# Moving and holding back the first tile's two stores in a streaming GELU-times kernel

## The chip, the cores and the metric

The kernel runs on one core of a Trainium2 chip. The metric is the device time of one execution in microseconds (us). Before the change it is 469.45 us, the median of 3 runs (469.33 to 469.8).

## The reference

The input is `x`, float32, of shape 32 × 512 × 2048. Each row of 2048 is cut in two halves of 1024: the first half goes through the exact GELU, and the result is multiplied by the second half.

```python
x1, x2 = (x[..., :half_dim].copy(), x[..., half_dim:].copy())
gelu_x1 = 0.5 * x1 * (1 + erf(x1 / np.sqrt(2)))
return (gelu_x1 * x2).astype(np.float32)
```

So 134.2 MB are read and 67.1 MB are written, and there is one activation and one product for every element of the output.

## The kernel before

The 16384 rows are cut into 16 tiles. A tile gives each of the 128 partitions 8 consecutive rows (R = 8), so a tile's load is 8 MB, 64 KB for each partition, and its store 4 MB, 32 KB for each partition. There are two input buffers and two output buffers, used in turn by even and odd tiles.

Four engines take part. SyncE only issues transfers: all the loads (line 47), and at the end the stores of tiles 14 and 15. ScalarE computes the GELU of a piece of a tile (line 81) and issues the other stores (line 54). VectorE multiplies the piece in place in the output buffer by the second half (line 89). Transfers issued by SyncE stand in one queue (q1 in the profile), those issued by ScalarE in another (q10); both are served by the same 16 DMA engines.

The order is written out by hand, with semaphores. Before the loop SyncE issues the two halves of tile 0 (rows 0 to 3 and 4 to 7, one semaphore each) and all of tile 1. In the loop:

- Tiles 0 and 15 are worked on in pieces of 2, 2 and 4 rows, all others in pieces of 5 and 3 rows (line 74). ScalarE waits for the tile's input before its first piece, and VectorE waits for each GELU (line 87).
- Every load of a tile and every store of the tile two before it count up the same semaphore, `ready[k]`, so ScalarE's first piece of tile i waits both for the load of tile i and for the store of tile i − 2, whose output buffer it will overwrite (line 79).
- A store waits until the products that it needs are counted in `mul_done` (line 52). The store of tile 0 is in two halves of 4 rows (2 MB each), issued by ScalarE after the second and after the third piece (line 101). Tile 15's is in two halves too, issued by SyncE. The others are whole (lines 103 to 106).
- After the products of tile i, SyncE issues the load of tile i + 2 into the buffer that has come free (lines 107 to 109).

A wait on an engine holds everything behind it on that engine: a store that ScalarE issues waits in ScalarE's own instruction order.

Of the kernel before, what the change touches and what calls it, by code (L numbers as in the profile page):

```python
# [1 line left out]

# [4 lines left out]

GELU = mybir.ActivationFunctionType.Gelu


@with_exitstack
def kernel(
    ctx: ExitStack,
    tc: tile.TileContext,
    x: bass.AP,
    out: bass.AP,
):
    nc = tc.nc
    P = nc.NUM_PARTITIONS

    x_flat = x.flatten_outer_dims()
    out_flat = out.flatten_outer_dims()
    n_rows, dim = x_flat.shape
    half = dim // 2

    R = 8
    x_t = x_flat.rearrange("(n p r) d -> n p r d", p=P, r=R)
    o_t = out_flat.rearrange("(n p r) d -> n p r d", p=P, r=R)
    n_tiles = x_t.shape[0]
    x_bufs = [nc.alloc_sbuf_tensor(f"x{k}_tile", [P, R, dim], x.dtype) for k in range(2)]  # L30
    o_bufs = [nc.alloc_sbuf_tensor(f"o{k}_tile", [P, R, half], out.dtype) for k in range(2)]

    first = [nc.alloc_semaphore(f"first{j}") for j in range(2)]
    ready = [nc.alloc_semaphore(f"ready{k}") for k in range(2)]
    gelu_done = nc.alloc_semaphore("gelu_done")
    mul_done = nc.alloc_semaphore("mul_done")
    tail_stored = nc.alloc_semaphore("tail_stored")
    n = {sem.name: 0 for sem in [*first, *ready, gelu_done, mul_done, tail_stored]}  # L40

    def counted(ins, sem, by):
        ins.then_inc(sem, by)
        n[sem.name] += by

    def load(i, rows, sem):
        ins = nc.sync.dma_start(out=x_bufs[i % 2][:, rows, :], in_=x_t[i][:, rows, :])  # L47
        counted(ins, sem, 16)
        return ins

    def store(queue, i, rows, sem):
        queue.wait_ge(mul_done, n[mul_done.name])
        counted(
            queue.dma_start(out=o_t[i][:, rows, :], in_=o_bufs[i % 2][:, rows, :]), sem, 16
        )

    for ins in (  # L60
        load(0, slice(0, 4), first[0]),
        load(0, slice(4, 8), first[1]),
        load(1, slice(0, 8), ready[1]),
    ):
        tc.no_tile_sem_insts.add(ins.ins.name)
    tc.close()
    tc.compile()  # L67

    for i in range(n_tiles):
        k = i % 2  # L70
        last = i == n_tiles - 1
        pieces = i == 0 or last
        steps = ((0, 2), (2, 4), (4, 8)) if pieces else ((0, 5), (5, 8))
        for lo, hi in steps:
            rows = slice(lo, hi)
            if i == 0 and lo % 4 == 0:
                nc.scalar.wait_ge(first[lo // 4], 16)
            elif lo == 0:
                nc.scalar.wait_ge(ready[k], n[ready[k].name])
            counted(  # L80
                nc.scalar.activation(  # L81
                    out=o_bufs[k][:, rows, :], in_=x_bufs[k][:, rows, :half], func=GELU
                ),
                gelu_done,
                1,
            )
            nc.vector.wait_ge(gelu_done, n[gelu_done.name])
            counted(
                nc.vector.tensor_mul(  # L89
                    out=o_bufs[k][:, rows, :],  # L90
                    in0=o_bufs[k][:, rows, :],
                    in1=x_bufs[k][:, rows, half:],
                ),
                mul_done,
                1,
            )
            if pieces and hi % 4 == 0:
                if last:
                    store(nc.sync, i, slice(hi - 4, hi), tail_stored)
                else:  # L100
                    store(nc.scalar, i, slice(hi - 4, hi), ready[k])
        if not pieces:
            if i == n_tiles - 2:
                store(nc.sync, i, slice(0, R), tail_stored)
            else:
                store(nc.scalar, i, slice(0, R), ready[k])
        if i + 2 < n_tiles:
            nc.sync.wait_ge(mul_done, n[mul_done.name])
            load(i + 2, slice(0, R), ready[k])


    nc.scalar.drain()  # L112
    for sem in (*first, *ready):
        nc.scalar.sem_clear(sem)
    nc.vector.drain()
    nc.vector.sem_clear(gelu_done)
    nc.sync.sem_clear(mul_done)
    nc.sync.wait_ge(tail_stored, n[tail_stored.name]).then_inc(
        tail_stored, -n[tail_stored.name]
    )  # L120


# [1 line left out]
_INS = ['x']  # L124
_OUTS = [((32, 512, 1024), 'float32')]


# [23 lines left out]
```

## Time and profile before

| | |
|---|---|
| time, median of 3 runs | 469.45 us (469.33 to 469.8) |
| span of the profiled execution | 467.9 us |
| VectorE busy | 140.5 us (30%), 34 instructions |
| ScalarE busy | 115.5 us (25%), 35 instructions |
| read and written | 134.22 MB and 67.11 MB, 430 GB/s over the span |
| transfers on SyncE's queue (q1) | 2880 packets, 142.61 MB |
| transfers on ScalarE's queue (q10) | 2160 packets, 58.72 MB |

The profile is of one execution, whose own time is not given apart from its span; the median of the runs lies 1.55 us above that span, for what goes on before the first and after the last recorded instruction. The page gives busy shares by engine, then the span in 40 slices, where a digit is the busy share in tenths (9 is 90% or more). A DMA queue's share is the time that its packets took, as a share of the span of all 16 engines. A line such as `47.20 4.48 ACT o_tile L81` of the chain gives the start, the duration, the engine, what it wrote, and the line of the kernel. `ACT <- DMA` in the list of waits reads: ScalarE waited for a transfer; the numbers are the sum, the count and the longest. ACTq and SPq are the engines' instruction queues, where transfers are issued.

### The profile page before, as it was taken

To read this page: it belongs to the slowest core of one execution; us is meant where nothing else is said; L and a number is where in the kernel's file an instruction comes from. 1 tells how busy PE (TensorE), PEld (TensorE's weight loads), DVE (VectorE), ACT (ScalarE), POOL (GpSimd) and SP (SyncE) were. 2 spreads that over 40 slices of the span, in tenths; PEclk is the share of its full clock that TensorE was granted. 3 is DMA by queue.
4 is the path that set the end of the run, shared out by engine and by line. 5 is a ranking of instruction groups with operands and counts; after the bars stand their busy time and mean duration, and the time that the engine had idled before them with its cause. 6 is when DMAs were issued, how large, how long until landed. Compare 5 with 4: busy or idle time off the path is not lost.

```text
span 467.9 us, 152 instructions
## 1 busy us (share of the span) xinstructions
DVE 140.5 (30%) x34; ACT 115.5 (25%) x35; POOL 0.2 (0%) x4
## 2 busy tenths in 40 slices
DVE  0330514207052060511606116060150702507043
ACT  1320606042060410604106050050500506014060
POOL 0000000000000000000000000000000000000000
DMA  8999999999999999999999999999999999999998
GB/s 359 448 448 443 403 405 492 409 403 448 459 437 403 434 417 493 403 403 448 476 420 403 445 406 493 403 406 445 487 409 403 445 451 448 403 434 417 493 389 373
DMA packets 5041, 201.34 MB, mean 430 GB/s; under 512 B 560, under 2 KB 560, under 8 KB 560
## 3 DMA queue, kind: packets, MB, share of 16 engines
q1 hardware_dynamic: 2880, 142.61, 70.6%
q10 hardware_dynamic: 2160, 58.72, 29.1%
q14 instruction: 1, 0.01, 0.0%
HBM read 134.22 MB, written 67.11 MB: 430 GB/s over the span
## 4 chain that ended last, share of the span: by engine, by line
DMA 76%; DVE 14%; ACT 8%; ACTq 0%; SPq 0%; issue 0%
DMA out_dram<-o_tile 66%; DVE o_tile L89 14%; DMA x_tile<-in_x_dram 10%; ACT o_tile L81 8%; ACTq L112 0%; SPq L47 0%
## 5 line engine op out<-in xcount | busy, mean ns | idle before, releaser
L89 DVE TENSOR_TENSOR o_tile<-o_tile,x_tile 128x5120 f32<-128x5120 f32 (+3 forms) x34 | 140.5, 4171 | 319.7 <-ACT o_tile L81 319.7
L81 ACT ACTIVATE o_tile<-x_tile 128x5120 f32<-128x5120 f32 (+3 forms) x34 | 114.3, 3407 | 337.4 <-DMA out_dram<-o_tile 301.6
L81 ACT ACT_TABLE_LOAD x1 | 1.3, 1283 | 2.9 <-PEq L67 2.9
L135 POOL MEMSET const-bfloat16-1.0<- 128x1 bf16 x1 | 0.1, 101 | 0.0
L135 POOL MEMSET const-uint8-127<- 128x1 uint8 x1 | 0.1, 101 | 0.0
L135 POOL MEMSET const-float32-0.0<- 128x1 f32 x1 | 0.1, 98 | 0.2 <-issue 0.2
L135 POOL MEMSET const-float32-1.0<- 128x1 f32 x1 | 0.1, 98 | 0.0
## 6 DMA issues: line engine op xcount, KB each, us to landing
out_dram<-o_tile ACTq DMA_DIRECT2D x13, 4096.0 KB, 44.7
x_tile<-in_x_dram SPq DMA_DIRECT2D x2, 4096.0 KB, 16.6
out_dram<-o_tile ACTq DMA_DIRECT2D x2, 2048.0 KB, 34.5
out_dram<-o_tile SPq DMA_DIRECT2D x1, 4096.0 KB, 25.2
out_dram<-o_tile SPq DMA_DIRECT2D x2, 2048.0 KB, 7.8
x_tile<-in_x_dram SPq DMA_DIRECT2D x15, 44.2
```

The costliest lines, as they stand in the source:

```text
L81: nc.scalar.activation(out=o_bufs[k][:, rows, :], in_=x_bufs[k][:, rows, :half], func=GELU),
L89: nc.vector.tensor_mul(out=o_bufs[k][:, rows, :], in0=o_bufs[k][:, rows, :], in1=x_bufs[k][:, rows, half:],),
L135: nc = _bacc.Bacc("TRN2", target_bir_lowering=False, num_devices=1)
```

## The change

Three things are changed around tile 0's stores and tile 1. Nothing else in the loop differs.

- Tile 0's first half store is issued by SyncE instead of ScalarE, so that it stands in q1 behind the load of tile 1, which was issued at the start, and ahead of the load of tile 2.
- Tile 0's second half store is still issued by ScalarE, but no longer right after tile 0's products. It comes after ScalarE's first piece of tile 1 in ScalarE's instruction order. It waits for the products of tile 0 only, whose count is kept in `done_0`.
- Tile 1 is worked on in pieces of 2, 3 and 3 rows instead of 5 and 3.

```diff
-    def store(queue, i, rows, sem):
-        queue.wait_ge(mul_done, n[mul_done.name])
+    def store(queue, i, rows, sem, done=None):
+        queue.wait_ge(mul_done, n[mul_done.name] if done is None else done)
...
         steps = ((0, 2), (2, 4), (4, 8)) if pieces else ((0, 5), (5, 8))
+        if i == 1:
+            steps = ((0, 2), (2, 5), (5, 8))
...
-            if pieces and hi % 4 == 0:
-                if last:
-                    store(nc.sync, i, slice(hi - 4, hi), tail_stored)
-                else:
-                    store(nc.scalar, i, slice(hi - 4, hi), ready[k])
+            if pieces and hi == 4 or last and hi == 8:
+                store(nc.sync, i, slice(hi - 4, hi), tail_stored if last else ready[k])
+            if i == 1 and lo == 0:
+                store(nc.scalar, 0, slice(4, 8), ready[0], done_0)
...
+        if i == 0:
+            done_0 = n[mul_done.name]
```

## The prediction

> **What bounds the kernel now.** I read the DMA part of the page first, because both compute engines are idle most of the span (DVE 30%, ACT 25%) and the chain of waits is 76% DMA.
>
> ```profile
> span 467.9 us, 152 instructions
> DMA  8999999999999999999999999999999999999998
> q1 hardware_dynamic: 2880, 142.61, 70.6%
> q10 hardware_dynamic: 2160, 58.72, 29.1%
> HBM read 134.22 MB, written 67.11 MB: 430 GB/s over the span
> ```
>
> q1 is SyncE's queue, q10 ScalarE's. Together their packets fill 99.7% of 16 engines' span. 70.6% of 467.9 is 330.3 us for 142.61 MB, 29.1% is 136.2 us for 58.72 MB: 0.432 and 0.431 MB/us. So a byte costs the same read or written and on either queue, and total bytes over that rate is nearly the whole time. The trace's packet records say the same in small: 64 KB takes 2.418 us, 32 KB 1.213, 16 KB 0.611, on both queues. A transfer is 144 packets, 9 on each engine: 8 of data and one 9 ns semaphore write. The first data packet starts at 1.74 us, the last ends at 467.4. Following the packets engine by engine I find no gap above 0.35 us, and what looks like gaps is cancelled by equally small overlaps: the 16 engines have no idle time to give back.
>
> Next the waits and the chain, to see what sets the phase.
>
> ```profile
> ACT o_tile L81 <- DMA out_dram<-o_tile: 301.6, 14, 21.9
> ACT o_tile L81 <- DMA x_tile<-in_x_dram: 35.7, 3, 21.1
> ```
> ```profile
> 47.20 4.48 ACT o_tile L81
> 51.70 8.77 DVE o_tile L89 x2
> 60.50 40.04 DMA out_dram<-o_tile
> 448.56 1.91 ACT o_tile L81
> 455.81 4.42 DVE o_tile L89
> ```
>
> From tile 2 on, ScalarE waits 14 times for the store of two tiles before. Yet the load of that tile lands only about one packet sooner, because the queues alternate packet by packet when both have work: in the steady part a 4 MB store is stretched to the 29.0 us of its 8 MB load (8 × 2.418 + 8 × 1.213 = 29.05). So the chain's "wait for a store" is the shared engines, and the windows view confirms it for two periods:
>
> ```profile
> 158.50:216.50 58.00, 17.52 (x4) 14.25 (x4) 0.00 (x0) 1.00 1.00 434
> ```
>
> (DVE, ACT, POOL busy, clock, DMA share, GB/s.) The timeline gives the start, the groups by shape the piece prices:
>
> ```profile
> 19.23 0.38 ACTq L54 DMA_DIRECT2D out_dram<-o_tile  x1
> 30.57 0.36 ACTq L54 DMA_DIRECT2D out_dram<-o_tile  x1
> ```
> ```profile
> L89 DVE TENSOR_TENSOR o_tile<-o_tile,x_tile 128x3072 f32<-128x3072 f32 x14 | 46.9, 3351 | 0.0
> L81 ACT ACTIVATE o_tile<-x_tile 128x3072 f32<-128x3072 f32 x14 | 38.5, 2747 | 0.0
> L89 DVE TENSOR_TENSOR o_tile<-o_tile,x_tile 128x2048 f32<-128x2048 f32 x4 | 9.0, 2288 | 32.4 <-ACT o_tile L81 32.4
> ```
>
> I write L0a, L0b, L1, L2... for loads and S0a, S0b, S1... for stores.
>
> **The change, part by part.**
>
> *S0a on SyncE's queue.* SyncE waits for the second product (about 19.2), issues S0a (0.35 us), then waits for the third (30.5) and issues L2 as before: the added wait holds nothing that could have gone sooner. In the ring the order is L0a, L0b, L1, S0a, L2. Bytes and packet prices are unchanged: 8 × 0.611 = 4.9 us per engine, spent after L1 instead of inside it. Cost 0. What the trace lacks is a store between two loads on one queue; the nearest rows are the end of the kernel, where L15, S14, S15a and S15b follow each other on q1: S14's first packet starts at 447.5, S15a's at 457.2, S15b's at 462.06, which is 8 × 1.21 and 8 × 0.61 with nothing between. Bounds 0 to 0.35 us (the largest gap found); I take 0.
>
> *L1 alone.* L1's first packet starts at 21.6 to 22.1 and took 2.7 us. With no stores in between, the other seven bring it to 21.9 + 2.7 + 7 × 2.418 = 41.5. L0b's last packet ended at 22.07 and ScalarE began on it at 22.46, so 0.4 later: tile 1 starts near 41.9 instead of 47.20. That is 5.3 us earlier, but only because 4.9 us of store work and the packets around it were put off.
>
> *Tile 1 in three pieces.* One ACTIVATE and one product more. ScalarE 1.90 + 2 × 2.75 = 7.40 against 7.22; VectorE 2.29 + 2 × 3.35 = 8.99 against 8.84: 0.18 and 0.15 us. ScalarE's pieces end at 43.8, 46.6 and 49.3, so VectorE runs 43.8 to 46.1, 46.6 to 50.0, 50.0 to 53.3. S1 and L3 are issued at 53.3, 7.2 us before the 60.5 of now. The cover is L2, which keeps q1 busy past 70; were it gone the extra would be 0.3 us.
>
> *S0b held back.* Its wait (third product) was met at 30.5, so it costs nothing in itself; queued behind it on ScalarE are only tile 1's other pieces. It is issued between 41.9 (ScalarE's queue runs ahead of its arithmetic: the drain L112 stands in the chain at 450.48, while gelus of tile 15 still follow) and 43.8 (after the first piece). An issue takes 1.0 us to its first packet (first load: 0.73 to 1.74) and at most 1.8 (S15b: 460.23 to 462.06). S0a now came in behind the packet in flight and one more; add that, 1.2 us if they are S0a's and up to 3.0 if one is L2's. So S0b's first packet starts between 44.1 and 48.6. In the early case it alternates with S0a's last packets, finishes before L2, and S1 takes its place beside L2: L2 ends up to 5 us later, tile 2 starts near 75 instead of 71.57, but waits for its load, with three or so packets of S1 already done. In the late case it pairs with L2's eight packets, the pattern of now, and tile 2 starts near 71. Both have the same bytes moved at each time, so the engines' account is equal: 0.
>
> *Does a queue run dry later?* The next load is issued at the end of a tile's products, some 13.3 us after its start, while the load of the following tile has 15 us or more left in q1. This holds in both phases.
>
> *The tail.* When tile 15 starts, S14 (8 × 1.21 = 9.7 us) and S15a, S15b (4.9 each) remain. S15a is issued 6.4 us into the tile, S15b 11.7 us (448.56 to 460.23). With 1.0 to 1.8 us they are in the rings 7.4 to 8.2 and 12.7 to 13.5 after the start. In the early case tile 15 starts 0.4 after L15's last packet, with S13 long done, and the turns come at 9.3 and 14.2: 0.7 us or more of slack. In the phase of now S14 has begun by the time S13 lands, and S15b's slack is 0 to 0.8 us (460.23 + 1.0 to 1.8 against 462.06). Neither opens a gap.
>
> The skill's page "DMA: Bandwidth & Descriptors", section "Anatomy of one DMA", speaks against the move: it fits a fixed cost of about 2.0 us to each DMA, most of it the write receipt. The four transfers back to back on q1 above show 0 between them instead; by the page, S0a in front of L2 would add an estimated 2.0 us, giving about 471.4.
>
> **Sum.** 0 for the bytes, 0 for the queue, 0 for the pieces, 0 for the tail; plus or minus 0.4. A gain has a small source: L1's packets beside the stores average 2.464 us, 0.37 us over eight, of which most is the slow first one that stays; 0.1 might go. The span stays 467.9 (467.5 to 468.3); the median of the runs lies 1.55 above that (469.45), so 469.4.
>
> **Rivals.**
>
> *S0b comes too late, and the tail opens: slower.* Each packet by which q10 lags q1 is kept from tile to tile, since both queues stay full. At the end it makes tile 15 start 1.21 us later while S14's packets go ahead of it; after the 0 to 0.8 us slack this is idle time. One packet more than now costs 0.4 to 1.2 us, two 1.6 to 2.4: 469.9 to 471.8. It decides (0.9 us) from about two packets on, that is, if S0b's first packet starts after 49 to 51. For it: the arbitration when S0b arrives isn't in the trace. Against: that is 2 us beyond my late bound.
>
> *The store in the load queue stalls it: slower.* Some switching time around S0a, or a ring that blocks SyncE's issue of L2. No row has its price; one packet's time on each engine bounds it, 0.6 to 2.4 us, so 470.0 to 471.8, over the limit from 0.9 us. Against: no gap at L15 to S14, and three transfers already wait in q1 at the start.
>
> *Unmixed transfers run faster: faster.* If reads alone beat the mix, the 20 us of L1 would shrink; 5% of it is 1.0 us, 468.4. Against: L0b, read alone, has its packets 1.21 us apart, the same as in the mix.
>
> **How the numbers follow.** About 0.2% (0.9 us) is what can be told from no change. The forecast's case: 0.76. Late S0b 0.09, of which 0.06 over the limit and 0.03 within it; stall 0.08, counted as all over. Unmixed transfers faster 0.07. So slower 0.14, same 0.79, faster 0.07. The range 468.7 to 470.5 holds the forecast's case and the one-packet lag, leaving out about 0.17: the two-packet lag (0.06), the stalls above 1 us (0.05) and most of the rate gain (0.06).
>
> **What would show it.** Right: tile 1's first ACTIVATE near 42 instead of 47.2; S1 and L3 issued near 53.3; q1 near 71.6% and q10 near 28.1% (one 2 MB store moved, 4.9 us of 467.9); their sum still 99.7%; DMA digits 9 to the last slice; the wait for a load taking over from the wait for a store if S0b was early. Wrong: digits below 9 near slice 4 (a stall around S0a), or in slices 39 and 40 with tile 15 starting after 449.8 (the late lag); a q1 share that grows without bytes would mean slower packets.

## The result, and the profile after

The changed kernel takes 470.24 us (median of 20 runs, 470.0 to 471.66), the kernel before 469.33 us (20 runs, 469.13 to 469.82). The ratio is 1.0020, with a 95% interval of 1.0014 to 1.0027: slower by 0.66 to 1.27 us. The forecast was 469.4 us and no change; the time is inside the range given, the sign is that of a rival.

The page of the changed kernel, the lines that answer to those shown of before:

```profile
span 469.0 us, 154 instructions
DMA  8999989999999999999999999999999999999998
GB/s 358 447 447 345 491 383 442 481 408 402 486 430 422 405 447 447 442 408 433 422 442 447 414 442 470 391 430 492 402 442 408 447 447 442 408 425 430 442 433 372
...
q1 hardware_dynamic: 3024, 144.70, 71.7%
q10 hardware_dynamic: 2016, 56.62, 28.0%
```

The same row of the kernel before:

```profile
GB/s 359 448 448 443 403 405 492 409 403 448 459 437 403 434 417 493 403 403 448 476 420 403 445 406 493 403 406 445 487 409 403 445 451 448 403 434 417 493 389 373
```

The queue shares are close to those worked out (71.6% and 28.1%), and together they still fill 99.7% of the engines' span. But the span is longer with the same bytes, so the engines were "busy" 1.1 us more for nothing. The DMA digits don't show where: the fourth slice (35 to 47 us) keeps its 9, and the 8 in the sixth comes from counting each packet in the slice in which it starts; in the packet records no engine is idle there. The GB/s row points to the place: its fourth slice has 345, where the kernel before has 443.

The start of the chain and the timeline of the changed kernel (start, duration, what):

```profile
1.64 41.64 DMA x_tile<-in_x_dram
...
54.56 49.28 DMA out_dram<-o_tile
...
449.41 1.91 ACT o_tile L83
```
```profile
43.30 1.91 ACT L83 ACTIVATE o_tile<-x_tile 128x2048 f32<-128x2048 f32 x1 [17.06 <-DMA x_tile<-in_x_dram]
43.31 0.38 ACTq L54 DMA_DIRECT2D out_dram<-o_tile  x1
...
54.56 0.36 ACTq L54 DMA_DIRECT2D out_dram<-o_tile  x1
74.85 7.12 ACT L83 ACTIVATE o_tile<-x_tile 128x5120 f32<-128x5120 f32 x2 [24.33 <-DMA out_dram<-o_tile]
```

Tile 1 starts at 43.30, not at the 41.9 worked out: 1.4 us late, though no store's packet came between those of the load. Everything after that keeps the forecast's shape, shifted: S1 and L3 are issued at 54.56 (53.3 was expected), tile 2 starts at 74.85 (near 75 in the early case), and tile 15 at 449.41 against 448.56 before.

The windows view around the end of L1 shows the place. A packet is counted in the window in which it starts (columns: window, length, DVE, ACT and POOL busy, clock, DMA share, GB/s):

```profile
36.00:38.00 2.00, 0.00 (x0) 0.00 (x0) 0.00 (x0) 1.00 1.21 524
38.00:40.00 2.00, 0.00 (x0) 0.00 (x0) 0.00 (x0) 1.00 1.90 524
40.00:42.00 2.00, 0.00 (x0) 0.00 (x0) 0.00 (x0) 1.00 0.00 0
42.00:44.00 2.00, 0.00 (x0) 0.70 (x1) 0.00 (x0) 1.00 0.88 377
```

From 38 to 40 us every engine starts L1's last packet: the same 524 GB/s as in the window before, but 1.90 instead of 1.21 of busy time. From 40 to 42 us no packet starts at all. In the packet records all 16 of these packets take 3.45 to 3.99 us instead of 2.418, on average 1.38 us more, and the next packet on each engine is the first of S0a. In the kernel before, the packets just ahead of S0a's first (L1's first ones) take 0.28 us more on average. That is the one large difference between the two traces. Stretched packets sum to 0.42 us per engine before and 1.42 after (counting what each data packet took beyond 2.418, 1.213 or 0.611 us and leaving out the very first packets, which take 0.6 us more in both), while the spans differ by 1.1.

### The profile page after: what moved, and what is told of

Same layout as the page of the kernel before. It is cut to its first block, busy times and chain, and to the rows that moved or that the text cites. A ratio compares the mean times of both kernels' runs of the same rounds, so it can differ in the third digit from the quotient of the medians.

```text
span 469.0 us, 154 instructions
## 1 busy us (share of the span) xinstructions
DVE 140.6 (30%) x35; ACT 115.6 (25%) x36; POOL 0.2 (0%) x4
## 4 chain that ended last, share of the span: by engine, by line
DMA 76%; DVE 14%; ACT 8%; issue 0%; ACTq 0%; SPq 0%
DMA out_dram<-o_tile 67%; DVE o_tile L91 14%; DMA x_tile<-in_x_dram 9%; ACT o_tile L83 8%; ACTq L117 0%; SPq L47 0%
## 5 line engine op out<-in xcount | busy, mean ns | idle before, releaser
L91 DVE TENSOR_TENSOR o_tile<-o_tile,x_tile 128x3072 f32<-128x3072 f32 (+3 forms) x35 | 140.6, 4057 | 320.4 <-ACT o_tile L83 320.4
L83 ACT ACTIVATE o_tile<-x_tile 128x3072 f32<-128x3072 f32 (+3 forms) x35 | 114.4, 3315 | 338.1 <-DMA out_dram<-o_tile 306.3
```

Source lines behind the costliest of these rows:

```text
L83: nc.scalar.activation(out=o_bufs[k][:, rows, :], in_=x_bufs[k][:, rows, :half], func=GELU),
L91: nc.vector.tensor_mul(out=o_bufs[k][:, rows, :], in0=o_bufs[k][:, rows, :], in1=x_bufs[k][:, rows, half:],),
```

## The experiments

The theory was that the stretch belongs to the first store behind a load in SyncE's queue. The questions: does it come from the queue, from its lateness, from being first, or is it the hold of S0b or the pieces that cost? In the table "stretch" is that sum per engine. Span and stretch are of the one profiled execution, whose own time is not the median: it was 471.74 us with S0a moved alone and 476.41 us with the pieces of 5 and 3.

| kernel | median us | ratio to before (95%) | span of profile | stretch |
|---|---|---|---|---|
| before | 469.3 | 1 | 467.9 | 0.42 |
| changed | 470.24 | 1.0020 (1.0014 to 1.0027) | 469.0 | 1.42 |
| S0a moved, nothing else | 470.38 | 1.0028 (1.0014 to 1.0043) | 470.3 | 1.24 |
| S0b held, three pieces | 477.26 | 1.0163 (1.0140 to 1.0187) | 476.2 | 6.93 |
| S0b held, pieces 5 and 3 | 477.41 | 1.0169 (1.0156 to 1.0182) | 475.1 | 6.88 |
| three pieces only | 469.25 | 1.0000 (0.9991 to 1.0008) | 467.9 | 0.48 |
| both halves held, on ScalarE | 476.59 | 1.0166 (1.0138 to 1.0195) | 475.0 | 1.78 |
| all stores on SyncE | 474.63 | 1.0118 (1.0101 to 1.0135) | 473.1 | 2.98 |

### Each part of the change alone

Only S0a moved:

```diff
-                    store(nc.scalar, i, slice(hi - 4, hi), ready[k])
+                    store(nc.sync if hi == 4 else nc.scalar, i, slice(hi - 4, hi), ready[k])
```

> Only S0a goes to SyncE's queue behind L1; S0b stays on ScalarE right after tile 0's products, tile 1 in pieces of 5 and 3. The changed kernel's packet records show one place where it loses time: the packet just ahead of the first store packet of the execution, on all 16 engines, takes 1.38 us more than its kind (the last packet of L1); in the kernel before, the packet ahead of the first store takes 0.28 us more. Theory A (the stall belongs to the first store, and is large where it stands behind a load in the same queue): here the first store is S0b on ScalarE's queue near 31 us, so a small stall of about 0.3 us there, none before S0a: 469.3 us. Theory B (large because nothing had been written until 40 us): also 469.3. Rival C (any store behind L1 in SyncE's queue stalls, first or not): about 1.4 us at the end of L1, 470.2 to 470.5.

It measured 470.38 us, a ratio of 1.0028: the move alone costs as much as the whole change, against A and B as I had put them. The profiled execution, of 471.74 us, is one of four near 472; the other eight lie between 469.91 and 470.59. Its packet records are less plain than those of the changed kernel. There is 0.53 us on the packets ahead of S0b's first (34 us) and 0.25 us near S0a's (39 to 42 us, with S0b's packets between), 0.22 us more where S1 starts, and the engines end 1.6 us apart (0.5 before) with up to 0.6 us of idle time at the tail. So of C the sum is right, but its place is not the one in this record; a run of the usual length was not profiled.

Only the hold, with S0a left on ScalarE:

```diff
+        if i == 1:
+            steps = ((0, 2), (2, 5), (5, 8))
...
+            if i == 1 and lo == 0:
+                store(nc.scalar, 0, slice(4, 8), ready[0], done_0)
```

(S0b is no longer stored right after tile 0's products, as in the changed kernel)

> S0a as in the kernel before (ScalarE, near 19 us); S0b held back and tile 1 in pieces of 2, 3 and 3 as in the changed kernel. Theories A and B: the first store is the same as before, 0.28 us, so 469.3 us, and the hold and the pieces cost nothing. Rival D (the hold of S0b or the third piece costs the time): 470.2 us.

477.26 us: a loss of 8 us, far more than any theory had. To split it I ran the pieces alone and the hold with the old pieces:

```diff
+        if i == 1:
+            steps = ((0, 2), (2, 5), (5, 8))
```

> The kernel before, tile 1 in pieces of 2, 3 and 3 rows, nothing else. All theories: 469.3 us, no difference; the piece costs 0.2 us on engines that wait anyway.

469.25 us, ratio 1.0000: the pieces cost nothing, as every theory said.

```diff
-            steps = ((0, 2), (2, 5), (5, 8))
+            steps = ((0, 5), (5, 8))
```

(against the hold alone above)

> S0a as in the kernel before; S0b after ScalarE's first piece of tile 1, with the pieces 5 and 3 kept: the hold alone. The hold with three pieces measured 477.3 us. Theory G (the hold alone does it, by making ScalarE's queue lag one packet or more behind SyncE's for good): 476 to 478, with tile 15 starting 9 us later and long load packets in every period. Rival H (the hold together with the pieces): below 472.

477.41 us: it is the hold. Its chain (start, duration, what) shows tile 3 at 103.26, where before has 100.56, and a period of 58.7 us for the next two tiles; its windows a lower rate in the steady part.

```profile
60.42 42.81 DMA out_dram<-o_tile
103.24 0.02 issue
103.26 4.48 ACT o_tile L83
...
161.91 4.48 ACT o_tile L83
...
221.28 4.48 ACT o_tile L83
...
456.76 1.91 ACT o_tile L83
```
```profile
175.00:233.00 58.00, 16.15 (x5) 14.25 (x4) 0.00 (x0) 1.00 1.01 431
293.00:351.00 58.00, 16.33 (x5) 14.25 (x4) 0.00 (x0) 1.00 1.01 429
```

434 GB/s had been the rate of before in such a stretch. The DMA share stays at 1.01, so this isn't idle time: from L4 on, each load has some of its 64 KB packets stretched, 0.2 to 0.75 us per engine and tile, and the engines drift apart (the last packets of L15 start 2.7 us apart, 0.5 before). I had thought of idle time at the tail; that is 0.7 us of the 7.2 by which this span is longer than the one before. One more run was to make the lag larger:

```diff
-            if i == 1 and lo == 0:
+            if i == 1 and hi == R:
```

(against the run above)

> S0a as in the kernel before; S0b after ScalarE's second piece of tile 1 (pieces 5 and 3), 4.5 us later than the hold that measured 477.4 us. Theory G (the loss comes with ScalarE's queue lagging behind SyncE's, and grows with the lag): 478 or more, tile 2 starting after 76, and tile 15 after 457. Rival J (the long load packets of the shorter hold come from one alignment of the two queues, not from the lag as such): below 475, with packets of ordinary length.

477.47 us, but it did not test what it was meant to. Its timeline has the store where the shorter hold has it, 0.01 us after the tile's start:

```profile
47.00 4.47 ACT L83 ACTIVATE o_tile<-x_tile 128x5120 f32<-128x5120 f32 x1 [20.84 <-DMA x_tile<-in_x_dram]
47.01 0.34 ACTq L54 DMA_DIRECT2D out_dram<-o_tile  x1
51.38 2.75 ACT L83 ACTIVATE o_tile<-x_tile 128x3072 f32<-128x3072 f32 x1
```

ScalarE's queue issues a transfer ahead of two ACTIVATEs that stand before it. In this kernel "after the first piece" or "after the second" is no hold at all beyond the wait for L1; the run is a third measurement of the same hold. Whether a larger lag costs more stays open.

### Queue or lateness

Both halves late, but from ScalarE:

```diff
+                store(nc.scalar, 0, slice(0, 4), ready[0], done_0)
                 store(nc.scalar, 0, slice(4, 8), ready[0], done_0)
```

(against the changed kernel; S0a no longer stands behind L1)

> Both halves of tile 0 are stored by ScalarE after its first piece of tile 1, so the first store comes near 44 us, as late as in the changed kernel, but from the other queue, beside L2's packets. Theory A (same queue makes the stall large): about 0.3 us ahead of the first store, 469.3 us. Theory B (lateness, that is 40 us of reading alone, makes it large): about 1.4 us, 470.2 us. If it comes out between, both count. The queue lag may also grow, because both halves are late: the tail could then add 0.4 us or more, which would show as tile 15 starting after 449.5.

At the end of L1 this is a clean answer. The chain and the windows of this kernel:

```profile
1.64 40.35 DMA x_tile<-in_x_dram
...
42.44 48.38 DMA out_dram<-o_tile
90.81 0.02 issue
90.83 4.48 ACT o_tile L83
```
```profile
38.00:40.00 2.00, 0.00 (x0) 0.00 (x0) 0.00 (x0) 1.00 1.21 524
40.00:42.00 2.00, 0.00 (x0) 0.00 (x0) 0.00 (x0) 1.00 1.22 524
```

The same loads, alone in the same queue, land at 41.99 instead of 43.28, and no packet is long there; the only difference up to this point is that L2 and not S0a stands behind L1. The first store, at 46 us from ScalarE, lengthens the packet ahead of it by 0.24 us. So lateness alone (B) falls: 22 or 43 us of reading alone give the same 0.25 us when the store comes from ScalarE. The total, 476.59 us, has another cause, which was one of the rivals of the prediction in a stronger form. ScalarE's queue is now 16 packets behind, so tile 2 can't start until S0b lands at 90.8, 19 us later than before; the load that waits for tile 2's products comes too late, and SyncE's queue runs dry:

```profile
95.00:100.00 5.00, 4.66 (x1) 2.96 (x2) 0.00 (x0) 1.00 0.90 387
100.00:105.00 5.00, 4.09 (x2) 0.46 (x1) 0.00 (x0) 1.00 0.00 0
105.00:110.00 5.00, 0.96 (x1) 5.00 (x2) 0.00 (x0) 1.00 1.02 341
```

No packet starts from 100 to 105 us: about 5 us of idle engines, once. After it the engines are busy at only 341 GB/s. In the packet records the first packets of L4, at 105 us, are 1.14 us longer in sum per engine, and the packet after each of them is the first of S2, from ScalarE's queue. So a stretch of this size also stands late in the run, with no store in SyncE's queue; the first packets of the run, far from any store, are 0.6 us longer, so part of it may be the restart after idle time.

### First or every time

All stores in one queue:

```diff
-                    store(nc.scalar, i, slice(hi - 4, hi), ready[k])
+                    store(nc.sync, i, slice(hi - 4, hi), ready[k])
...
-                store(nc.scalar, i, slice(0, R), ready[k])
+                store(nc.sync, i, slice(0, R), ready[k])
```

> Every store goes on SyncE's queue, so there is one queue only: L0a, L0b, L1, S0a, S0b, L2, S1, L3, and so on, fifteen changes from a load to a store in one ring with nothing beside them. Theory A1 (each such change costs the 1.38 us of the changed kernel): 16 times that, 490 us or more. Theory A2 (only the first change costs it, 1.4 us ahead of S0a): 469.9 to 470.5. Rival E (the stall is in the meeting of two queues near 39 us, not in the ring): no stall, 469.0 to 469.4.

A stretch like that of the changed kernel, 1.28 us, is there again at the end of L1:

```profile
38.00:40.00 2.00, 0.00 (x0) 0.00 (x0) 0.00 (x0) 1.00 1.85 524
40.00:42.00 2.00, 0.00 (x0) 0.00 (x0) 0.00 (x0) 1.00 0.00 0
```

At the next fourteen changes from load to store the packets of the load are longer by 0 to 0.25 us, so a change of direction in a ring does not cost 1.4 us each time (A1 falls). The total, 474.63, lies between A2's 470.5 and A1's 490: the small stretches sum to 1.7 us, and the engines drift apart until at the tail the last ends 1.5 us behind the first, with 1.5 us of idle time between S14 and S15a.

A store of SyncE's queue later in the run:

```diff
-                store(nc.scalar, i, slice(0, R), ready[k])
+                store(nc.sync if i == 1 else nc.scalar, i, slice(0, R), ready[k])
```

> The kernel before with one edit: S1 goes on SyncE's queue, behind L2 and ahead of L3. S0a and S0b are stored by ScalarE as before. S1 is then the first store of SyncE's queue, with ScalarE's queue empty beside it, but not the first store of the execution. Theory A2 for the execution's first store: no stall, 469.3 to 469.5. Theory A2 for the queue's first store, or C (any store behind a whole load in that queue): 1.1 to 1.4 us at the end of L2, near 70 us, 470.2 to 470.6.

470.57 us (469.68 to 473.9, scattered), ratio 1.0032 (1.0015 to 1.0048). The profiled execution is the shortest of the ten (469.68 us, span 468.2) and has no long packet at the end of L2; one of S0b's packets still lay between there. It has 0.26 us ahead of S2, when ScalarE's queue fills again after a pause. What its slower runs lose isn't in the trace. In two more runs ScalarE's queue is empty at the end of the loads, because S0b is left out:

```diff
-                else:
+                elif hi == 4:
                     store(nc.scalar, i, slice(hi - 4, hi), ready[k])
```

> The kernel before without the store S0b (half of tile 0's output is left out, 2.1 MB or 4.9 us of the engines' time). ScalarE's queue is then ahead by eight packets, so it is empty at the end of L15, and S14, the first store of SyncE's queue, follows L15 with nothing in between. Theory X: no stall there, 469.3 less 4.9, 464.4 us, a ratio of 0.9896. Theory Y: 1.1 to 1.4 us more at the end of L15, 465.5 to 465.8, a ratio near 0.992.

464.79 us, ratio 0.9905 (0.9891 to 0.9919): 0.4 us above theory X's number, below Y's. The records have none of it at S14: L15's last packets take 2.42 us, and S14 follows at once, at 443 us, with ScalarE's queue empty. They have 0.22 us at 63 us, ahead of S1's first packet.

```diff
-                store(nc.scalar, i, slice(0, R), ready[k])
+                store(nc.sync if i == 2 else nc.scalar, i, slice(0, R), ready[k])
```

(against the run above)

> The kernel before without S0b (half of tile 0's output is left out; that alone measured 464.8 us, with ScalarE's queue empty at the end of every load and no stretched packet at S14) and with S2 on SyncE's queue behind L3. S2 is then the queue's first store, at about 96 us, alone, after several stores from ScalarE. Theory X (only the execution's first writes pay): no stretched packet at the end of L3, 464.6 to 465.0 us. Theory Y2 (the first store of SyncE's queue pays unless it comes at the very end): 1.1 to 1.4 us at the end of L3, 465.8 to 466.2.

465.13 us, again no stretch at the end of L3. The windows show it, with S2 starting near 95.3 and ScalarE's queue empty:

```profile
92.00:94.00 2.00, 0.00 (x0) 0.00 (x0) 0.00 (x0) 1.00 1.21 524
94.00:96.00 2.00, 0.00 (x0) 0.10 (x1) 0.00 (x0) 1.00 0.61 262
96.00:98.00 2.00, 0.00 (x0) 2.00 (x1) 0.00 (x0) 1.00 1.21 524
```

So that queue's first store is free at 95 us and at 443 us, with L3 or L15 alone ahead of it: the price at 39 us is not one that every first store in that queue pays. In both runs the packets at 63 us, ahead of S1 from ScalarE's queue, are longer, by 0.22 and 0.42 us.

### What an earlier store changes

Four runs put some of tile 0's output out earlier: S0a's first row from ScalarE (the other three rows behind L1), the same row from SyncE ahead of L1, all of S0a from SyncE ahead of L1, and 16 of the 128 partitions from ScalarE:

```diff
+                if not last:
+                    store(nc.scalar, 0, slice(0, 1), ready[0])
-                store(nc.sync, i, slice(hi - 4, hi), tail_stored if last else ready[k])
+                store(nc.sync, i, slice(hi - 4 if last else 1, hi), tail_stored if last else ready[k])
```

> As the changed kernel, but the first of S0a's four rows (0.5 MB) is stored by ScalarE near 19 us; the other three rows go on SyncE's queue behind L1. Theories A and B: the first store is now the early row, 0.3 us; S0a's rest behind L1 finds the path in use, no stall: 469.3 to 469.5 us. Rival C (any store behind L1 in that queue stalls): 1.4 us stays at the end of L1, 470.2 to 470.5.

470.11 us, ratio 1.0013 (1.0002 to 1.0024). L1's last packets are still 1.06 us longer. Theories A and B fail here: the execution's first store was earlier, in the other queue, and the stretch stayed. The packets just ahead of that early row, at 22 us, take 2.42 us, so it cost nothing itself.

```diff
-        load(1, slice(0, 8), ready[1]),
...
+            if i == 0 and lo == 0:
+                store(nc.sync, 0, slice(0, 1), ready[0])
+                load(1, slice(0, R), ready[1])
```

(the rest of S0a as in the run above)

> As the changed kernel, but the first of S0a's four rows goes on SyncE's queue ahead of L1 (L1 is issued right behind it, near 17 us, while L0b still runs), the other three behind L1. Theory A2 in the form that SyncE's queue pays for its own first store: the stall is now at the early row, near 22 us, and none ahead of S0a's rest: about 470 if it is as large there, 469.3 if small. Theory F (it is paid by what follows a whole 8 MB load in reading alone, first or not): 1.1 to 1.4 us at the end of L1, 470.1 to 470.4.

469.82 us, ratio 1.0012 (1.0003 to 1.0021). Now L0b's last packets, near 19 to 22 us and just ahead of the early row, are 1.11 us longer in sum per engine, and L1's last have nothing. L1's end shows it:

```profile
38.00:40.00 2.00, 0.00 (x0) 0.00 (x0) 0.00 (x0) 1.00 1.21 524
40.00:42.00 2.00, 0.00 (x0) 0.00 (x0) 0.00 (x0) 1.00 1.21 524
```

This kernel and the run above store the same row at nearly the same time (first packets at 22.8 and 24.1 us); the price is paid where SyncE's queue has its first store. L1 is also issued later here, behind the row, which the run does not separate from the queue. The same addresses were written early in both, so the place in the output is not the reason.

```diff
-                    store(nc.scalar, i, slice(hi - 4, hi), ready[k])
+                    store(nc.sync if hi == 4 else nc.scalar, i, slice(hi - 4, hi), ready[k])
+                    if hi == 4:
+                        load(1, slice(0, R), ready[1])
```

(S0a ahead of L1; L1 no longer issued at the start)

> S0a on SyncE's queue ahead of L1 instead of behind it (L1 is issued right after S0a, near 19.7 us, while L0b still runs to 22); S0b on ScalarE near 30.6 as in the kernel before, tile 1 in pieces of 5 and 3. The first store is then in the load queue, alone, after 20 us of reading instead of 40. Theory A2 (first store behind a load in its own queue costs 1.4): 470.2, with the stall near 22 us. Theory B (it grows with the time of reading alone, 0.28 at 22 us): 469.3.

471.30 us, ratio 1.0041 (1.0026 to 1.0057). The four times lie between 470.27 and 471.86, and the profiled one is 471.81. The stretch ahead of S0a is 0.53 us at 20 to 21 us, less than half of A2's 1.4; another 0.54 us come at 46 to 49 us, where S0b's packets lie among L1's, and the engines end 1.6 us apart.

```diff
+                if not last:
+                    store(nc.scalar, 0, slice(0, 4), ready[0], parts=slice(0, 16))
```

(partitions 16 to 127 behind L1 on SyncE)

> As the changed kernel, but 16 of S0a's 128 partitions (one 16 KB packet on each engine) are stored by ScalarE near 19 us; the other 112 go on SyncE's queue behind L1 as before. The early packet is through by 25 us, so at the end of L1 ScalarE's queue is empty. Theory X (the stall belongs to the first store of the execution): 0.3 us near 22 us, nothing at the end of L1: 469.3 to 469.5 us. Theory Y (it belongs to the first store in SyncE's queue, behind loads, when the other queue has no packet to put in between): 1.1 to 1.4 us at the end of L1 again, 470.2 to 470.5.

480.96 us, scattered from 472.89 to 485.79; the two shortest alone give a ratio of 1.010 (1.0082 to 1.0118). The profiled execution is one of the long ones, 480.58 us, so what it loses later is not explained here. In it the end of L1 has 0.41 us, neither X's 0 nor Y's 1.1. Its engines drift apart (the last packets of L15 start 3.8 us apart), and long packets follow in nearly every tile. It decides nothing between X and Y.

## Why the prediction was wrong

**The step that failed** is "S0a on SyncE's queue ... Cost 0", with its "Bounds 0 to 0.35 us". It measured 1.38 us on the packets ahead of S0a, 0.28 of which the kernel before already paid at its own first store, so 1.1 us net (1.0 in the sum of all stretched packets, 1.1 in the span). The nearest row had been L15, S14, S15a and S15b at the end of the kernel, and I misread it: in the packet records one packet of S13, 1.21 us from ScalarE's queue, lies on each engine between L15's last packet (ended by 446.8) and S14's first (from 447.5 on). So the row did not show a load followed at once by a store. Where S14 does follow L15 at once, at 448.4 us in the changed kernel and at 443 us in the one without S0b, it is free, and so is the mid-run store at 95 us. It was no price for the first store of the run. Also, I had looked for gaps between packets; what came is a longer packet, which counts as busy and leaves the digit of its slice at 9. One sign of being wrong did come: SyncE's queue took 336.2 us per engine in the packet records, 1.0 more than its bytes (330.3 and S0a's 4.9).

That the time still lies in the range is luck: the upper end was there for a lag of one packet, which did not occur. And the 1.55 us added to the span was 1.27 in the profiled execution (470.27 us, span 469.0), so the median rose by 0.9 us where the span rose by 1.1.

**The rival "the store in the load queue stalls it"** gave 470.0 to 471.8 and is what happened, in the form of a longer packet; SyncE's issue of L2 was not blocked (30.73 against 30.56 before). It had a chance of 0.08, held down by the argument from L15 and S14.

**S0b held back, "it costs nothing in itself"**: true inside the change, false alone (8 us). In the changed kernel S0b is issued at 43.31, 0.01 us after tile 1 starts, which was my early case, with S0a's packets still in SyncE's queue. ScalarE's queue then runs ahead of the loads, and steady periods are as before: 434 GB/s from 175.15 to 233.15. Without the move the same line lets that queue fall behind: S13's last packets end 2.8 us after L15's on average, with pieces of 5 and 3, where the kernel before has 1.2. That the packets alternate in an unlucky order there is argued from the records, not shown.

**The pieces, 0**: right (ratio 1.0000). **Tile 1 alone, 41.9**: 42.01 measured in the kernel without a store behind L1; the changed kernel's 43.30 is this plus the stretch. **The tail without a gap**: right. The wait list should have gone over to loads; it still names stores, 14 times. The packet records have S13's last packet end 5.4 us before L15's, but load and store count the same semaphore, and the list can't tell them apart.

**The late lag** did not occur in the change, but both halves held showed that it is real, and earlier than I had put it: a dry load queue at 100 us and not the tail.

**The 2.0 us for each DMA** of the Trainium skill's page "DMA: Bandwidth & Descriptors", section "Anatomy of one DMA", which by itself would have given 471.4, is not what the runs show either: 1.1 to 1.4 us once, 0 to 0.25 at the next changes, none at 95 and 443 us. The page fits that figure to transfers issued by GpSimd (its SWDGE path) and puts most of it down to completion; this kernel issues none from GpSimd, so it was no price for S0a.

**What stays open.** Why the packets lengthen is not shown. In the opening of the run, up to about 40 us, every stretch of over 1 us stands ahead of the first store of SyncE's queue, S0a or its early row. A later first store there is free; an early row from ScalarE removes little of it (1.38 to 1.06), 16 early partitions more (0.41, in a run of 480.58 us), and its size varies from 0.25 to 1.4 us. The 1.14 us at 105 us, with both halves held, has no store in SyncE's queue at all. No single rule of those tried fits all of them. No version here that stores everything beats the kernel before, whose engines have 0.4 us of stretched packets and no idle time to win back.

## What to carry to other kernels

Where the transfer engines are never idle, a new order of the same transfers has little to win: none of those tried here is faster, and most are slower. Look then for which packets a reordering lengthens, and compare packet durations or GB/s by slice, since busy shares hide it. A price taken from a like pattern at another time of the run is not a bound for the start of the run; read it packet by packet, to see that nothing of another queue lies between. Measure the parts of a combined edit alone before calling one of them free: here one part costs 8 us alone and nothing beside the other.

## What was not expected of the hardware

- Ahead of the first store of SyncE's queue, in the first 40 us, packets of the load are longer: by 1.38 us on all 16 engines in the changed kernel, 1.28 with all stores in that queue, 1.06 and 1.11 with an early row, 0.53 with S0a ahead of L1, and less (0.41 and 0.25) in two long runs. Ahead of the first store of ScalarE's queue it is 0 (an early row) to 0.5 us (S0b, with S0a moved).
- A transfer that stands behind one or two ACTIVATEs in ScalarE's order, its wait already met, is issued 0.01 us after the first of them starts (43.31 after 43.30, 47.01 after 47.00).
- With S0b held back alone, 64 KB packets become longer by 0.2 to 0.75 us per tile for the rest of the run, without idle time before the tail (431 and 429 instead of 434 GB/s), and the engines drift 2.7 us apart.
